# Memory rows transposed ahead of their scaling, and gate sums by triangle products, in a streaming encoder step

## The chip, the cores and the metric

The kernel runs on one core of a Trainium2 chip. The metric is the device time of one execution in microseconds (us). Engines are named as in the profile: PE (TensorE matmuls; PEld its weight loads), DVE (VectorE), ACT (ScalarE), POOL (GpSimd) and SP (SyncE, which here issues all the DMAs; SPq is its queue in the timeline).

## The reference

One inference step of a one-layer trunk in fp32: 1024 new frames of one stream and 16 new frames of each of 8 running streams, 1024 features. Three mixers run side by side on the normalised rows (stick-breaking attention, a Mamba-2 group, and forgetting attention), then cross-attention into 256 memory rows and a SwiGLU FFN. The change touches the memory rows' keys and values, and the running sums of the forget gates:

```python
def rmsnorm(x, g):
    xf = x.astype(jnp.float32)
    y = xf * lax.rsqrt(jnp.mean(xf * xf, axis=-1, keepdims=True) + EPS)
    return (y * g.astype(jnp.float32)).astype(x.dtype)

def mem_kv(mem, g, wk, wv):
    mn = rmsnorm(mem, g)
    k = jnp.einsum('bmd,de->bme', mn, wk) ...
    v = jnp.einsum('bmd,de->bme', mn, wv) ...

# in mixers(): new frames of the prompt, then of the running streams
logf = jax.nn.log_sigmoid((fg + p['fox_b_f']).astype(jnp.float32))
fcum = jnp.cumsum(logf, axis=1)
fcum = jnp.cumsum(jnp.concatenate([past['fox_logf'], logf], axis=1), axis=1)

# in fox_attend()
s = s + (fq[..., :, None] - fk[..., None, :])      # both are fcum
```

The cache holds 1024 past rows of four heads' log gates for each of 8 streams.

## The kernel before, in words

The program is written for a framework that orders the instructions of each engine by a simulated timeline and by priorities set in the code; each engine then runs its list in order, and a waiting instruction holds all that stand behind it on its engine. SP's DMAs take turns on eight semaphores, so that a DMA also waits for the one eight before it. Buffers come from pools: `st` for raw weights at the start, `ring` (tags `wh` and `wl`, three buffers each; `wr`, two) for weights, cached keys (`kf`) and cached values (`vr`).

Products keep fp32 accuracy by splitting each operand into a rounded high part and the rest: mm3 (L314 to L316) is high times high, high times low, low times high. A weight's high part is a cast on ACT (L289), the rest a subtraction in pieces of 256 columns on POOL (L132).

*The start.* L140 loads the 256 memory rows in two halves of 128x1024; L143 and L144 load six rows of gains, the convolution's bias and its taps, which PE turns into columns (L219). mem_proj (L783) normalises the memory rows by norm_T (L258): squares on ACT (L265), the root by rstd_of (L249 to L255, POOL and DVE), the scaling on DVE (L269), then eight times two transposes (L275), a copy to the high part with the gain (ACT, L276) and the low part (DVE, L277). Sixteen units of two 128x512 weight tiles of wk_x and wv_x follow, 12 products each; four units make one output, copied out on ACT (L804). Between the units come pieces of `aux`: norm_T for nine blocks of the x rows, with the same lines, from `ws` tiles.

*The gate sums.* fill_s (L1200) hands out work that fills PE's gaps while the stick-breaking pipeline runs: the last projections, then fox_sums (L646), pad_cols (transposes L756), and in the order `ORD` the first half of the z projection (products L314 to L316 of 264 columns), the convolution's columns, and z's second half. fox_sums stores the log gates (L650, L651), transposes the prompt's to rows (L657), scans 4x1024 (DVE, L659), stores the sums as `fcsc`, transposes them back (L663) into `fqc`. It gathers the cached gates (L669, 8192 runs of four floats), puts them in order (L672), transposes to rows (L678), adds the new frames' (L681, L685), scans 32x1040 (DVE, L687) and stores the rows 16 times over to DRAM as `fssc` (L688). L692 to L697 make `fnew`. Later the decode units of the forgetting attention read `fssc` back into `fkb` (L877), and four small loads (L1211, `fqs`) read the new frames' sums from it.

Beside this run the pipeline's rows (scores on PE L547 to L550; sigmoids on ACT L504 and L505 into `ws`; a scan on DVE, L507; a product on POOL, L132; transposes L565, copies to `pt` L568, products with values L580; the heads' output is stored to `mixsc` by L596) and the decode units: cached keys loaded (L851), transposed (L857), copied (L858), multiplied (L844), their weights transposed (L891, L892) and multiplied with the cached values (loads L909, products L900).

Of the kernel before, what the change touches and what calls it, by code (L numbers as in the profile page):

```python
# [62 lines left out]
def tile_hybrid_step(ctx: ExitStack, tc: tile.TileContext, a: dict):  # L63
# [22 lines left out]
    def act_t(dt=F32R, home=None):  # L86
        return (home or actp).tile([P, 3072], dt, tag="act", name="act")
# [4 lines left out]
    def st_t(dt=F32R):  # L92
        return stp.tile([P, 1024], dt, tag="st", name="st")
# [4 lines left out]
    def xc_t(dt=F32):  # L98
        return xcp.tile([P, 1056], dt, tag="xc", name="xc")
# [10 lines left out]
    def pd():  # L110
        return ps_t(psd, "d")
# [4 lines left out]
    def pT():  # L116
        return ps_t(pst, "t")
# [17 lines left out]
        return sm.tile([P, 16], dt, tag="sm", name="sm")[:, :n]  # L135


    xm = act_t(F32)
    for i in range(2):
        SP.dma_start(out=xm[:, i * D:(i + 1) * D], in_=a["mem_prompt"][0, i * P:(i + 1) * P, :])  # L140
    rows = xc_t()
    for i, g in enumerate(("norm_mix_g", "norm_x_g", "norm_ffn_g", "mem_norm_g", "conv_b")):
        SP.dma_start(out=rows[8 * i:8 * i + 8, :P], in_=a[g][0].rearrange("(k p) -> k p", p=P))  # L143
    SP.dma_start(out=rows[40:72, :P], in_=a["conv_w"][0].rearrange("i (k p) -> (i k) p", p=P))  # L144
    first_raw = []
    for k0 in (0, 2):
# [69 lines left out]


    colp = pT()
    PE.transpose(colp[:, :72], rows[:72, :P], ident[:72, :72])  # L219
    cols = cst.tile([P, 72], F32, name="cols")  # L220
    DVE.tensor_copy(cols, colp[:, :72])
    DVE.tensor_scalar(cols[:, 32:72], cols[:, 32:72], 0.5, None, ALU.mult)
    g_mix, g_x, g_ffn, g_mem = (cols[:, 8 * i:8 * i + 8] for i in range(4))
    conv_b = cols[:, 32:40]

    hb = mcst.tile([P, 28], F32, name="hb")
    lf = mcst.tile([P, NBLK, 4], F32, name="lf")
# [10 lines left out]
    mix_sc = dram([8, 2, P, T], F32R, "mixsc")  # L238
    o_sc = dram([8, 2, P, T], F32R, "osc")
    fc_sc = dram([4, SEQ], F32, "fcsc")  # L240
    fs_sc = dram([32, DEC_S, PAST + DEC_S], F32, "fssc")
    ac_sc = dram([72, P], F32, "acsc")
    mk_sc = dram([256, D], F32, "mksc")
    mv_sc = dram([256, D], F32, "mvsc")
# [401 lines left out]
    def fox_sums():  # L646
        l = log1p_exp_negabs(lf, [P, NBLK, 4])
        DVE.scalar_tensor_tensor(lf.rearrange("p a b -> p (a b)"), lf.rearrange("p a b -> p (a b)"), 0.0,
                                 l.rearrange("p a b -> p (a b)"), ALU.min, ALU.subtract)
        SP.dma_start(out=a["p_fox_logf"][0, 0].rearrange("(k p) h -> p k h", p=P), in_=lf[:, 0:8, :])  # L650
        SP.dma_start(out=a["s_fox_logf"][0].rearrange("b q h -> (b q) h"), in_=lf[:, 8, :])  # L651

        fr = xc_t()
        for hf in range(2):
            tp = pd()
            for b in range(4):
                PE.transpose(tp[:4, b * P:(b + 1) * P], lf[:, 4 * hf + b, :], ident)  # L657
            ACT.copy(fr[0:4, hf * 512:(hf + 1) * 512], tp[:4])
        DVE.tensor_tensor_scan(fr[0:4, :SEQ], fr[0:4, :SEQ], fr[0:4, :SEQ], 0.0, ALU.add, ALU.bypass)  # L659
        SP.dma_start(out=fc_sc, in_=fr[0:4, :SEQ])  # L660
        tp = pd()
        for b in range(8):
            PE.transpose(tp[:, b * 4:(b + 1) * 4], fr[0:4, b * P:(b + 1) * P], ident[:4, :4])  # L663
        DVE.tensor_copy(fqc, tp[:, :32].rearrange("p (b h) -> p b h", h=4))
        yield


        pl0 = sg_t()[:, :256]
        SP.dma_start(out=pl0.rearrange("p (u h) -> p u h", h=4),  # L669
                     in_=a["cache_fox_logf"][0].rearrange("b k h -> (b k) h").rearrange("(u p) h -> p u h", p=P))  # L670
        pl1 = sg_t()[:, :256]
        DVE.tensor_copy(pl1.rearrange("p (k b h) -> p k b h", k=8, h=4),  # L672
                        pl0.rearrange("p (b k h) -> p k b h", k=8, h=4))
        sr = xc_t()[0:32, :PAST + DEC_S]
        for hf in range(2):
            tp = pd()
            for b in range(4):
                PE.transpose(tp[:32, b * P:(b + 1) * P], pl1[:, (4 * hf + b) * 32:(4 * hf + b + 1) * 32], ident)  # L678
            ACT.copy(sr[:, hf * 512:(hf + 1) * 512], tp[:32])
        x8 = sg2_t()  # L680
        DVE.tensor_tensor(out=x8[:, :32].rearrange("p (b h) -> p b h", h=4),  # L681
                          in0=lf[:, 8, :].unsqueeze(1).to_broadcast([P, 8, 4]),
                          in1=smask.unsqueeze(2).to_broadcast([P, 8, 4]), op=ALU.mult)
        tp = pd()
        PE.matmul(tp[:32, :16], x8[:, :32], fold, start=True, stop=True)  # L685
        ACT.copy(sr[:, PAST:], tp[:32, :16])
        DVE.tensor_tensor_scan(sr, sr, sr, 0.0, ALU.add, ALU.bypass)  # L687
        SP.dma_start(out=fs_sc, in_=sr.unsqueeze(1).to_broadcast([32, DEC_S, PAST + DEC_S]))  # L688
        yield
# [93 lines left out]
    def mem_proj(xm, aux):  # L783

        mh, ml = act_pair(256)
        drain(norm_T([xm[:, i * D:(i + 1) * D] for i in range(2)], g_mem, lambda: (mh, ml), 256, xm[:, 2 * D:]))
        work = [(a[wname][0], j, k0, sc, out) for wname, sc, out in (("wk_x", mk_sc, "p_mem_k"), ("wv_x", mv_sc, "p_mem_v"))
                for j in range(2) for k0 in (0, 2, 4, 6)]
        nxt = [[t[:, :1024].rearrange("p (k n) -> p k n", n=512) for t in split_unit(raw, 1024)] for raw in first_raw]
        for n, (w, j, k0, sc, out) in enumerate(work):  # L790
            wh, wl = nxt.pop(0)
            if n + 2 < len(work) :
                w2, j2, k2 = work[n + 2][:3]
                nxt.append(w_unit([(w2, j2 * 512, 512)], k2, 2, st_t(F32)))
# [12 lines left out]
            next(aux, None)  # L807

    def decode_units(m):
# [15 lines left out]
        def rows(p):  # L827
# [372 lines left out]
    def fill_s():  # L1200
        yield from dense_T(w_in, uc, [(C_FQ, consume_qk(4, 0, QS))])
        yield from dense_T(w_in, uc, [(C_FQ + P, consume_qk(5, 1, QS))])
        yield from dense_T(w_in, uc, [(C_FK, consume_qk(6, 0, None, p_k[1], s_k[1]))])
        yield from dense_T(w_in, uc, [(C_FK + P, consume_qk(7, 1, None, p_k[1], s_k[1]))])
        yield from proj_v(1, C_FV, p_v[1], s_v[1], extra=4)
        yield from fox_sums()
        pad_cols()
        for o in ORD:
            if o == "z1":
                for p in range(4):  # L1210
                    SP.dma_start(out=fqs[:, p:p + 1], in_=fs_sc[8 * p:8 * p + 8, 0, PAST:PAST + DEC_S])  # L1211
# [777 lines left out]
```

## Time and profile before

| | |
|---|---|
| median of 3 runs | 1927.26 us (1920.28 to 1929.67) |
| the profiled execution's own time | 1923.12 us |
| its span in the trace | 1921.4 us |
| mean granted TensorE clock | 0.983 |
| PE busy | 1842.2 us |
| PE's waits in 0 to 76 us | 12.3 us |
| PE's waits in 270 to 335 us | 14.8 us |
| bytes moved by DMA | 307.52 MB |

The rows shown below are of five kinds. Waits: engine, tile and line that waited, what released it, us in total, times, longest. Timeline: start in us, duration, engine, line, operation, written tile, read tiles, shapes, and how often in a row; in brackets the idle time ahead of it and what ended it. Stretches: from and to, length, then busy time and instructions of PE, PEld, DVE, ACT and POOL, the granted clock, the DMA engines' busy share and GB/s. For SPq a timeline row's length is the time that the queue needed to hand the DMAs over, waits included. The page's head gives each engine's busy time and share of the span. The clock of a stretch is a record of the throttle.

### The profile page before, as it was taken

How to read it: one execution, taken by the hardware profiler on the slowest of the kernel's cores; microseconds unless marked ns; L12 is line 12 of the kernel's file. 1: busy time of each engine (PE TensorE's matmuls, PEld its weight loads, DVE VectorE, ACT ScalarE, POOL GpSimd, SP SyncE). 2: the span in 40 equal slices, each digit the busy share in tenths (PEclk: the TensorE clock that was granted, in tenths of full speed). 3: DMA queues.
4: the chain of work that ended last, by engine and by line, in shares of the span. 5: the costliest groups of instructions: out<-in, count | busy, mean ns of one | idle time of the engine just before them, and what ended most of it. 6: DMA issues, size and time to landing. Idle time of an engine off the chain costs nothing.

```text
span 1921.4 us, 32161 instructions
## 1 busy us (share of the span) xinstructions
PE 1842.2 (96%) x12128; PEld 1644.5 (86%) x12128; DVE 900.7 (47%) x1803; ACT 818.1 (43%) x1716; POOL 629.2 (33%) x915
## 2 busy tenths in 40 slices
PE   7989997989999899999999999999999999999998
PEld 5889776888986777899998889999999999888886
DVE  3421324365746883354435387333333433455555
ACT  6431543444656772243333175333333333344343
POOL 7632406154323663211101214554444443000000
PEclk9999996999999999999999999999999999999999
DMA  9454647445588887444558123322323223566572
GB/s 335 142 169 155 213 120 177 131 113 161 162 259 260 273 296 242 143 143 143 184 183 302 66 91 98 93 69 69 86 77 80 69 69 96 192 197 238 174 239 94
DMA packets 304778, 307.52 MB, mean 160 GB/s; under 512 B 88684, under 2 KB 259796, under 8 KB 304624
## 3 DMA queue, kind: packets, MB, share of 16 engines
q1 hardware_dynamic: 304624, 305.48, 51.5%
q8 instruction: 95, 1.56, 0.3%
q14 instruction: 59, 0.48, 0.1%
HBM read 229.31 MB, written 76.11 MB: 159 GB/s over the span
## 4 chain that ended last, share of the span: by engine, by line
PE 77%; DMA 7%; DVE 4%; POOL 3%; ACT 2%; issue 2%; SPq 1%; DVEq 0%; POOLq 0%; ACTq 0%
PE psd L1811 11%; PE psd L314 9%; PE psd L315 9%; PE psd L316 9%; PE pst L1811 8%; PE pss L1811 4%; PE pss L314 3%; PE pss L315 3%; PE pss L316 3%; DMA act<-acsc 2%; PE pso L1811 2%; PE pst L314 1%; PE pst L315 1%; PE pst L316 1%; PE pso L580 1%
## 5 line engine op out<-in xcount | busy, mean ns | idle before, releaser
L132 POOL TENSOR_TENSOR wl<-wr,wh 128x256 fp32r<-128x256 f32 (+1 forms) x180 | 139.0, 805 | 223.5 <-ACT wh L289 172.8
L314 PE MATMUL psd<-act,wh 128*128 128x384 f32 x576 | 198.0, 344 | 4.6 <-DVE sg L441 2.6
L316 PE MATMUL psd<-act,wl 128*128 128x384 f32 x576 | 196.7, 342 | 0.1
L315 PE MATMUL psd<-act,wh 128*128 128x384 f32 x576 | 196.2, 341 | 0.0
L1811 PE MATMUL pst<-bT,tr 128*128 128x256 f32 (+1 forms) x1068 | 155.0, 293 | 0.0
L1811 PEld LDWEIGHTS pst<-bT,tr 128*128 128x128 f32 x1068 | 144.9, 188 | 0.1
L316 PE MATMUL psd<-wh,act 128*128 128x512 f32 (+3 forms) x424 | 137.8, 326 | 0.0
L314 PE MATMUL psd<-wh,act 128*128 128x256 f32 (+3 forms) x414 | 134.9, 329 | 2.3 <-DMA act<-osc 1.1
L315 PE MATMUL psd<-wl,act 128*128 128x256 f32 (+3 forms) x414 | 135.2, 328 | 0.5 <-POOL wl L132 0.5
L1811 PE MATMUL psd<-bT,tr 128*128 128x320 f32 (+1 forms) x912 | 132.9, 295 | 0.7 <-DVE tr L1658 0.5
L1811 PEld LDWEIGHTS psd<-bT,tr 128*128 128x128 f32 x912 | 124.7, 188 | 1.2 <-DVE tr L1658 0.7
L132 POOL TENSOR_TENSOR ws<-ws 128x256 f32<-128x256 f32 (+2 forms) x100 | 74.3, 772 | 137.7 <-DVE ws L507 115.1
L314 PEld LDWEIGHTS psd<-act,wh 128*128 128x128 f32 x576 | 108.6, 188 | 10.7 <-DVE sg L441 3.0
L132 POOL TENSOR_TENSOR tr<-u,tr 128x256 fp32r<-128x256 f32 x110 | 83.3, 786 | 98.1 <-ACT tr L1654 80.3
L316 PEld LDWEIGHTS psd<-act,wl 128*128 128x128 f32 x576 | 108.4, 188 | 2.1 <-issue 1.5
L315 PEld LDWEIGHTS psd<-act,wh 128*128 128x128 f32 x576 | 108.6, 189 | 0.6 <-issue 0.4
L251 POOL TENSOR_SCALAR sm<-sm 128x1 f32<-128x1 f32 (+2 forms) x27 | 9.0, 335 | 300.2 <-ACT y L1894 209.4
L1786 DVE TENSOR_TENSOR tr<-tr,pst 128x256 f32<-128x256 f32 (+1 forms) x86 | 38.6, 449 | 138.2 <-ACT tr L1783 105.1
L132 POOL TENSOR_TENSOR tr<-raw,tr 128x256 fp32r<-128x256 f32 x94 | 69.3, 765 | 85.9 <-ACT tr L1654 77.7
L1654 ACT CAST tr<-tr 128x384 fp32r<-128x384 f32 (+1 forms) x70 | 37.7, 538 | 122.5 <-DMA tr<-hidsc 112.3
L314 PEld LDWEIGHTS psd<-wh,act 128*128 128x128 f32 x414 | 80.2, 194 | 10.6 <-issue 1.3
L289 ACT CAST wh<-wr 128x1024 fp32r<-128x1024 f32 (+2 forms) x45 | 46.7, 1050 | 97.6 <-PE psd L316 35.2
(609 smaller groups left out, 4713.2 us busy)
## 6 DMA issues: line engine op xcount, KB each, us to landing
u<-w_down SPq DMA_DIRECT2D x40, 512.0 KB
raw<-w_down SPq DMA_DIRECT2D x26, 512.0 KB
st<-qksc SPq DMA_DIRECT2D x48, 256.0 KB
wr<-w_in SPq DMA_DIRECT2D x22, 512.0 KB
tr<-hidsc SPq DMA_DIRECT2D x57, 192.0 KB
hidsc<-tr SPq DMA_DIRECT2D x34, 288.0 KB
qksc<-sg SPq DMA_DIRECT2D x48, 192.0 KB
wr<-cache_sb_k SPq DMA_DIRECT2D x16, 512.0 KB
```

The source lines that it names most:

```text
L132: POOL.tensor_tensor(out=out[:, a0:a1], in0=in0[:, a0:a1], in1=in1[:, a0:a1], op=op)
L251: POOL.tensor_scalar(v, ss, inv, EPS, ALU.mult, ALU.add)
L289: ACT.copy(hi[:, :n], raw[:, :n])
L314: PE.matmul(out, ah, bh, start=start, stop=False)
L315: PE.matmul(out, ah, bl, start=False, stop=False)
L316: PE.matmul(out, al, bh, start=False, stop=stop)
L580: return PE.matmul(po[r:r + 64, q_], vt[:, 2 * (k0 + i) + j, :], pfs[i][:, sl], start=start and k0 == 0 and (j == 0 or qp > 0), stop=k0 + ...
L1654: ACT.copy(hi, src)
L1786: DVE.tensor_tensor(out=at(out, g), in0=at(x, g), in1=ps[g][:, :GW[g]], op=op)
L1811: PE.matmul(dst[g][:, :GW[g]], x[:, ka], y[:, k, :], start=start and k == 0 and m == 0, stop=stop and k == 3 and m == 2, skip_group_check= ...
```

## The change

*Start.* The loads are put in the order memory half 1, five rows of gains and bias, first weights, memory half 2, three more weights, the taps. The memory rows are transposed as they are; the copies to the high and low parts apply the gain; squares and root are taken after the first unit, and the root scales the copy-out of each product (`ACT.activation(t, ps[i], AF.Copy, scale=...)`). The taps become columns after the second unit. Weights are loaded four units ahead instead of two. Units 0, 1, 2, 5, 8, 11 and 14 take their low part on DVE in one subtraction of 1024 columns instead of four on POOL.

*Gate sums.* Sums within a block of 128 rows are products with a triangle of ones, sums of earlier blocks products of running column sums (small additions on DVE) with a matrix of ones. The prompt's sums come out as columns (`fqc`) and are transposed to rows for `fcsc`; the cached ones come out as rows. A scan of 16 columns remains. `fssc` holds two copies instead of 16, and `fkb` reads each eight times.

*Order of the fqs loads.* They are kept in program order.

```diff
-    xm = act_t(F32)
-    for i in range(2):
+    xm, rows = act_t(F32), xc_t()
...
+    load_xm(0)
     for i, g in enumerate(("norm_mix_g", "norm_x_g", "norm_ffn_g", "mem_norm_g", "conv_b")):
         SP.dma_start(out=rows[8 * i:8 * i + 8, :P], in_=a[g][0].rearrange("(k p) -> k p", p=P))
...
+    load_wk(0)
+    load_xm(1)
+    for n in range(1, 4):
+        load_wk(n)
+    SP.dma_start(out=rows[64:96, :P], in_=a["conv_w"][0].rearrange("i (k p) -> (i k) p", p=P))
...
-    fs_sc = dram([32, DEC_S, PAST + DEC_S], F32, "fssc")
+    fs_sc = dram([32, 2, PAST + DEC_S], F32, "fssc")
...
+        pl0, pl1 = sg_t(), sg_t()
+        SP.dma_start(out=pl0[:, :256].rearrange("p (u h) -> p u h", h=4),
+                     in_=a["cache_fox_logf"][0].rearrange("b k h -> (b k) h").rearrange("(u p) h -> p u h", p=P))
+        triu, ones = pl1[:, 256:384], pl1[:, 384:512]
...
+        for b in range(1, 7):
+            DVE.tensor_tensor(out=pre[:, 4 * b + 4:4 * b + 8], in0=pre[:, 4 * b:4 * b + 4], in1=lf[:, b, :], op=ALU.add)
+        tp = pd()
+        PE.matmul(tp[:, :32], triu, lf[:, 0:8, :].rearrange("p b h -> p (b h)"), start=True, stop=False)
+        PE.matmul(tp[:, 4:32], ones, pre[:, 4:32], start=False, stop=True)
+        DVE.tensor_copy(fqc.rearrange("p b h -> p (b h)"), tp[:, :32])
...
-        DVE.tensor_tensor_scan(fr[0:4, :SEQ], fr[0:4, :SEQ], fr[0:4, :SEQ], 0.0, ALU.add, ALU.bypass)
...
-            PE.transpose(tp[:, b * 4:(b + 1) * 4], fr[0:4, b * P:(b + 1) * P], ident[:4, :4])
...
+                PE.matmul(o, pp[:, k * 32:(k + 1) * 32], triu, start=True, stop=k == 0)
+                if k:
+                    PE.matmul(o, ps_[:, k * 32:(k + 1) * 32], ones, start=False, stop=True)
...
-        DVE.tensor_tensor_scan(sr, sr, sr, 0.0, ALU.add, ALU.bypass)
-        SP.dma_start(out=fs_sc, in_=sr.unsqueeze(1).to_broadcast([32, DEC_S, PAST + DEC_S]))
-        yield
+        DVE.tensor_tensor_scan(n8, n8, n8, 0.0, ALU.add, ALU.bypass)
+        DVE.tensor_scalar(sr[:, PAST:], n8, sr[:, PAST - 1:PAST], None, ALU.add)
+        SP.dma_start(out=fs_sc, in_=sr.unsqueeze(1).to_broadcast([32, 2, PAST + DEC_S]))
...
-        drain(norm_T([xm[:, i * D:(i + 1) * D] for i in range(2)], g_mem, lambda: (mh, ml), 256, xm[:, 2 * D:]))
...
+                    for t in split_unit(first_raw.pop(0), 1024, DVE if n < 2 or n % 3 == 2 else POOL)]
...
+            ACT.activation(mh[:, k, :], tp[:, :256], AF.Copy, scale=g_mem[:, k:k + 1])
+            DVE.scalar_tensor_tensor(ml[:, k, :], tp[:, :256], g_mem[:, k:k + 1], f32(mh[:, k, :]), ALU.mult, ALU.subtract)
...
-                    ACT.copy(t, ps[i])
+                    ACT.activation(t, ps[i], AF.Copy, scale=rstd[0][:, i:i + 1])
...
+            if n == 0:
+                root()
+            if n == 1:
+                tap_columns()
...
-            SP.dma_start(out=fkb[:, :PAST], in_=fs_sc[8 * p:8 * p + 8, :, :PAST].rearrange("i t k -> (i t) k"))
+            SP.dma_start(out=fkb[:, :PAST],
+                         in_=fs_sc[8 * p:8 * p + 8, :, :PAST].rearrange("i c k -> (i c) k").unsqueeze(1)
+                         .to_broadcast([16, DEC_S // 2, PAST]))
...
-                    SP.dma_start(out=fqs[:, p:p + 1], in_=fs_sc[8 * p:8 * p + 8, 0, PAST:PAST + DEC_S])
+                    tc.keep_in_program_order(
+                        SP.dma_start(out=fqs[:, p:p + 1], in_=fs_sc[8 * p:8 * p + 8, 0, PAST:PAST + DEC_S]))
```

The change also moves instructions that it doesn't name. On SP, where the gate sums begin, before (L851 loads cached keys, L306 the z columns of w_in, L669 gathers the cached gates):

```order
L851 DMA wr<-cache_sb_k 128x1024 x2
L669 DMA sg<-cache_fox_logf 128x64x4
L596 DMA mixsc<-sg 64x2x256
L306 DMA wr<-w_in 128x4x256
L306 DMA wr<-w_in 128x4x8
L306 DMA wr<-w_in 128x4x256
L306 DMA wr<-w_in 128x4x8
L650 DMA p_fox_logf<-lf 128x8x4
L651 DMA s_fox_logf<-lf 128x4
```

and now (L668 is the gather, L910 the keys, L664 and L665 the stores of the gates, L320 w_in):

```order
L668 DMA sg<-cache_fox_logf 128x64x4
L910 DMA wr<-cache_sb_k 128x1024 x2
L610 DMA mixsc<-sg 64x2x256
L664 DMA p_fox_logf<-lf 128x8x4
L665 DMA s_fox_logf<-lf 128x4
L320 DMA wr<-w_in 128x4x256
L320 DMA wr<-w_in 128x4x8
L320 DMA wr<-w_in 128x4x256
L320 DMA wr<-w_in 128x4x8
```

The gather went from behind the two key loads to ahead of them, and the two stores of the gates from behind the w_in loads to ahead of them.

On ACT at the same place, before (L858 copies transposed keys, L568 transposed weights of the pipeline, L658 the gates' rows; L289 is the cast of w_in's z columns):

```order
L858 COPY kf<-pst 128x512 x4
L568 COPY pt<-pst 128x512 x2
L504 ACTIVATE ws<-pss 128x512
L505 ACTIVATE ws<-pss 128x512
L504 ACTIVATE ws<-pss 128x128
L505 ACTIVATE ws<-pss 128x128
L658 COPY xc<-psd 4x512 x2
L568 COPY pt<-pst 128x384
L289 CAST wh<-wr 128x1056
```

and now (L917, L582, L518, L519 and L303 are the former L858, L568, L504, L505 and L289; L693 copies the sums' rows):

```order
L917 COPY kf<-pst 128x512 x4
L303 CAST wh<-wr 128x1056
L582 COPY pt<-pst 128x512 x2
L693 COPY xc<-psd 4x512 x2
L303 CAST wh<-wr 128x1056
L518 ACTIVATE ws<-pss 128x512
L519 ACTIVATE ws<-pss 128x512
L518 ACTIVATE ws<-pss 128x128
L519 ACTIVATE ws<-pss 128x128
L582 COPY pt<-pst 128x384
```

Both casts went ahead, the first of them ahead of the copies of the pipeline's weights. POOL's list follows: both splits of w_in's z columns now stand ahead of the product of the decode unit's 1152-column row, which was ahead of the first and is now behind the second. On PE three score rows of the pipeline (256, 384 and 512 columns) went from ahead of the z projection to behind its first blocks.

On SP behind the sums' store, before (L688 stores `fssc`, L1211 the four `fqs` loads, L769 stores z, L909 loads cached values):

```order
L688 DMA fssc<-xc 512x1x1040
L851 DMA wr<-cache_sb_k 128x1024
L1211 DMA fqs<-fssc 128x1x1 x2
L769 DMA zsc<-sg 128x256
L1211 DMA fqs<-fssc 128x1x1 x2
L909 DMA vr<-cache_sb_v 128x1024 x2
```

and now:

```order
L720 DMA fssc<-xc 64x1x1040
L800 DMA zsc<-sg 128x256
L970 DMA vr<-cache_sb_v 128x1024 x2
L506 DMA st<-qksc 64x1024
L507 DMA st<-qksc 64x1024
```

The `fqs` loads are gone from here; they stand some 90 rows further on in SP's list. The key load went ahead of the store. Towards the out-projection a few instructions on each engine trade places; none is added there. From the cross-attention on, the lists are alike.

More of the change, by code (lines that the diff above doesn't have):

```diff
@@ L218, in tile_hybrid_step, with tap_columns @@
     colp = pT()
-    PE.transpose(colp[:, :72], rows[:72, :P], ident[:72, :72])
+    PE.transpose(colp[:, :40], rows[:40, :P], ident[:40, :40])
     cols = cst.tile([P, 72], F32, name="cols")
-    DVE.tensor_copy(cols, colp[:, :72])
-    DVE.tensor_scalar(cols[:, 32:72], cols[:, 32:72], 0.5, None, ALU.mult)
+    DVE.tensor_copy(cols[:, 0:40], colp[:, :40])
+    def tap_columns():
+        tp = pT()
+        PE.transpose(tp[:, :32], rows[64:96, :P], ident[64:96, 64:96])
+        DVE.tensor_copy(cols[:, 40:72], tp[:, :32])
+        DVE.tensor_scalar(cols[:, 32:72], cols[:, 32:72], 0.5, None, ALU.mult)
     g_mix, g_x, g_ffn, g_mem = (cols[:, 8 * i:8 * i + 8] for i in range(4))
@@ L226, in tile_hybrid_step @@
     hb = mcst.tile([P, 28], F32, name="hb")
+    xm_r = mcst.tile([P, 2], F32, name="xm_r")
     lf = mcst.tile([P, NBLK, 4], F32, name="lf")
@@ L656, in fox_sums @@
             for b in range(4):
-                PE.transpose(tp[:4, b * P:(b + 1) * P], lf[:, 4 * hf + b, :], ident)
+                PE.transpose(tp[:4, b * P:(b + 1) * P], fqc[:, 4 * hf + b, :], ident)
             ACT.copy(fr[0:4, hf * 512:(hf + 1) * 512], tp[:4])
-        DVE.tensor_tensor_scan(fr[0:4, :SEQ], fr[0:4, :SEQ], fr[0:4, :SEQ], 0.0, ALU.add, ALU.bypass)
         SP.dma_start(out=fc_sc, in_=fr[0:4, :SEQ])
[L661 to L664, printed above, removed]
-        yield
[L668 to L679, printed above, removed]
+        DVE.tensor_copy(ps_[:, 32:64], pp[:, 0:32])
+        for k in range(1, 7):
+            sl = slice(32 * k, 32 * k + 32)
+            DVE.tensor_tensor(out=ps_[:, 32 * k + 32:32 * k + 64], in0=ps_[:, sl], in1=pp[:, sl], op=ALU.add)
         x8 = sg2_t()
@@ L785, in mem_proj, with unit, root @@
         mh, ml = act_pair(256)
-        drain(norm_T([xm[:, i * D:(i + 1) * D] for i in range(2)], g_mem, lambda: (mh, ml), 256, xm[:, 2 * D:]))
         work = [(a[wname][0], j, k0, sc, out) for wname, sc, out in (("wk_x", mk_sc, "p_mem_k"), ("wv_x", mv_sc, "p_mem_v"))
                 for j in range(2) for k0 in (0, 2, 4, 6)]
-        nxt = [[t[:, :1024].rearrange("p (k n) -> p k n", n=512) for t in split_unit(raw, 1024)] for raw in first_raw]
+        def unit(n):
+            return [t[:, :1024].rearrange("p (k n) -> p k n", n=512)
+                    for t in split_unit(first_raw.pop(0), 1024, DVE if n < 2 or n % 3 == 2 else POOL)]
+        nxt = [unit(0)]
+        for k in range(KT):
+            tp = pT()
+            for i in range(2):
+                PE.transpose(tp[:, i * P:(i + 1) * P], xm[:, i * D + k * P:i * D + (k + 1) * P], ident)
+            ACT.activation(mh[:, k, :], tp[:, :256], AF.Copy, scale=g_mem[:, k:k + 1])
+            DVE.scalar_tensor_tensor(ml[:, k, :], tp[:, :256], g_mem[:, k:k + 1], f32(mh[:, k, :]), ALU.mult, ALU.subtract)
+        nxt.append(unit(1))
+        ss, rstd = small(2), []
+        def root():
+            for i in range(2):
+                ACT.activation(xm[:, 2 * D:], xm[:, i * D:(i + 1) * D], AF.Square, accum_out=ss[:, i:i + 1])
+            r = xm_r[:, 0:2]
+            DVE.tensor_copy(r, rstd_of(ss, 2, 1.0 / D))
+            rstd.append(r)
         for n, (w, j, k0, sc, out) in enumerate(work):
             wh, wl = nxt.pop(0)
-            if n + 2 < len(work) :
-                w2, j2, k2 = work[n + 2][:3]
-                nxt.append(w_unit([(w2, j2 * 512, 512)], k2, 2, st_t(F32)))
+            if n + 4 < len(work):
+                w2, j2, k2 = work[n + 4][:3]
+                first_raw.append(st_t(F32))
+                SP.dma_start(out=first_raw[-1].rearrange("p (k n) -> p k n", n=512),
+                             in_=w2[k2 * P:(k2 + 2) * P, j2 * 512:(j2 + 1) * 512].rearrange("(k p) n -> p k n", p=P))
+            if n + 2 < len(work):
+                nxt.append(unit(n + 2))
             if k0 == 0:
```

33 lines of the change are left out of this document (24 added, 9 removed).

## The prediction

> **What bounds the kernel now.** I read the page's head first, then PE's waits in the two places that the change touches, then the busy time by stretch there, and the timeline where a wait had to be explained.
>
> ```profile
> span 1921.4 us, 32161 instructions
> PE 1842.2 (96%) x12128; PEld 1644.5 (86%) x12128; DVE 900.7 (47%) x1803; ACT 818.1 (43%) x1716; POOL 629.2 (33%) x915
> ```
>
> PE is busy for 1842.2 of 1921.4 us, so only PE's idle time, and PE's work at a reduced clock, can be won. The profiled execution took 1923.12 us; the median of the three runs is 1927.26, 4.1 above it. I sum against 1923.12 and add 4.1. A difference under 0.5% (9.6 us) is about what a measurement of this kernel cannot tell from no change.
>
> PE's waits in 0 to 76 us, then in 270 to 335 us (total, times, longest):
>
> ```profile
> PE pst L219 <- DMA xc<-conv_w: 6.6, 1, 6.6
> PE pst L275 <- DVE act L269: 3.0, 2, 2.8
> PE pst L275 <- DVE act L277: 1.3, 2, 0.9
> PE pst L275 <- DVE ws L269: 0.9, 2, 0.5
> ```
>
> ```profile
> PE pss L547 <- ACT ws L505: 4.3, 1, 4.3
> PE pso L900 <- DMA vr<-cache_sb_v: 3.5, 1, 3.5
> PE pst L857 <- DMA wr<-cache_sb_k: 2.0, 2, 1.1
> PE psd L663 <- DVE xc L659: 1.7, 1, 1.7
> ...
> PE pss L547 <- ACT xc L686: 0.8, 1, 0.8
> PE pst L891 <- POOL ws L132: 0.7, 1, 0.7
> ```
>
> The start idles 11.8 us in these, the gate sums and the decode unit beside them some 13. The busy time by stretch (length, then PE, PEld, DVE, ACT, POOL, then granted clock, DMA share, GB/s) shows what those gaps draw after them:
>
> ```profile
> 28.00:72.00 44.00, 42.10 (x200) 33.30 (x200) 18.04 (x25) 30.37 (x46) 43.67 (x61) 1.00 0.63 226
> 293.40:313.90 20.50, 14.69 (x62) 12.49 (x60) 11.89 (x12) 7.34 (x18) 20.50 (x27) 0.50 0.85 203
> 313.90:324.20 10.30, 8.24 (x95) 7.59 (x93) 2.06 (x4) 1.90 (x5) 2.76 (x7) 1.00 0.63 181
> 324.20:334.40 10.20, 8.28 (x62) 7.73 (x63) 1.51 (x7) 2.99 (x6) 2.79 (x4) 0.50 0.59 160
> ```
>
> Behind the gaps PE ran at half clock twice, for 20.5 and 10.2 us; half of the busy time there was lost. POOL was saturated in 28 to 72 us and in 293.4 to 313.9.
>
> **The start.** Timeline, 0 to 14 us:
>
> ```profile
> 4.60 1.06 ACT L265 ACTIVATE act<-act 128x1024 f32<-128x1024 f32 x1 [2.54 <-DMA act<-mem_prompt]
> 5.96 1.06 ACT L265 ACTIVATE act<-act 128x1024 f32<-128x1024 f32 x1 [0.20 <-DMA act<-mem_prompt]
> 8.02 1.04 ACT L289 CAST wh<-st 128x1024 fp32r<-128x1024 f32 x1 [0.91 <-DMA st<-wk_x]
> 8.88 1.89 DVE L269 TENSOR_SCALAR act<-act,sm 128x1024 f32<-128x1024 f32 x2
> 11.87 0.80 PE L314 MATMUL psd<-wh,act 128*128 128x512 f32 x1
> ```
>
> The two halves of the memory rows were there by 4.60 and 5.96. Squares, root and DVE's scaling (to 10.77) stood between them and the transposes, and the first product came at 11.87. The change takes that chain out. The second half now lands behind one 512 KB weight load, which I estimate from 5.96 - 4.60 = 1.36 us: 7.3. Then comes a transpose, the copy on ACT (behind a 1.04 us cast, and perhaps one square of 1.06): first product between 8.3 and 9.7. I take 9.2, a gain of 2.7. Fewer waits for the transposes of the x rows, whose scaling stood in DVE's queue beside mem's (1.3 + 0.9, of which I take half), add 1.1. POOL gives 28 of its pieces to DVE. There a subtraction of 1024 columns costs between 0.95 (the scaling above, 1.89 for two) and four POOL pieces; DVE is busy 18.04 of 44 us, so 7 of them hide. The root's squares now run on ACT beside products, and hide unless the first eviction comes before them, 48 products later. Sum 3.8, as **-4**; -6 if the squares stay out of the way, 0 if ACT's order holds the copies.
>
> **The gate sums.** SP, ACT and PE, by the timeline:
>
> ```profile
> 276.27 1.15 SPq L851 DMA_DIRECT2D wr<-cache_sb_k  x2
> 277.46 0.43 SPq L669 DMA_DIRECT2D sg<-cache_fox_logf  x1
> 278.00 6.76 SPq L596 DMA_DIRECT2D mixsc<-sg  x1
> 285.19 2.10 SPq L306 DMA_DIRECT2D wr<-w_in  x4
> 287.34 0.52 SPq L650 DMA_DIRECT2D p_fox_logf<-lf  x1
> 287.90 2.21 SPq L651 DMA_DIRECT2D s_fox_logf<-lf  x1
> ```
>
> ```profile
> 280.30 1.06 PE L857 MATMUL pst<-ident,wr 128*128 128x128 f32 x8 [0.97 <-DMA wr<-cache_sb_k]
> 282.43 1.07 PE L857 MATMUL pst<-ident,wr 128*128 128x128 f32 x8 [1.07 <-DMA wr<-cache_sb_k]
> 287.18 1.08 PE L580 MATMUL pso<-pt,st 128*64 128x256 f32 x8
> 299.63 0.58 PE L547 MATMUL pss<-st 128*128 128x256 f32 x1 [0.78 <-ACT xc L686]
> 305.72 0.80 PE L547 MATMUL pss<-st 128*128 128x512 f32 x1 [4.34 <-ACT ws L505]
> 308.49 0.59 PE L314 MATMUL psd<-wh,act 128*128 128x264 f32 x1
> ```
>
> ```profile
> 289.47 1.07 ACT L289 CAST wh<-wr 128x1056 fp32r<-128x1056 f32 x1 [0.63 <-DMA wr<-w_in]
> ```
>
> ```profile
> 286.26 0.29 DVE L672 COPY sg<-sg 128x256 f32<-128x256 f32 x1 [4.09 <-DMA sg<-cache_fox_logf]
> ```
>
> Against it: the gather of 8192 runs of 16 B held SP's queue for 6.76 us, landing at 286.26; it now stands ahead of the two key loads. The last keys, at 282.43 now, come 3.8 later if both share the bytes (286.26), 2.3 if half of the hold is the keys' own bytes, 6.8 if the whole hold falls on them. And the two stores of L650 and L651 (0.52 + 2.21 = 2.7) now stand ahead of the w_in loads, whose cast ran at 289.47 and now comes at 292.2. The cast is now ahead of the two copies to pt in ACT's queue: pt is ready at 292.2 + 1.07 + 1.1 = 294.4, so PE's L580 moves from 287.18 to 294.4. That covers the late keys too.
>
> For it: from there to the z projection before took 308.49 - 287.18 = 21.3. Of this the waits of 1.7, 0.8, 0.7 and 4.3 are 7.5; the 4.3 belongs to a score row that the change moves behind z blocks, with two others whose products, from 299.63 to about 301.4, took 1.75 at half clock. The scan and its transposes back go, 15 products of 32x128 come; I set them equal. So z starts at 294.4 + 21.3 - 7.5 - 1.75 = 306.5, 2.0 earlier. POOL allows it: it splits both halves of w_in first, then its 1152-column product. The moved rows come back at 0.9, at full clock: **-1**, between -5 (keys and casts at once) and +6 (the hold falls on both).
>
> **The clock.** In these rows PE fell to half clock at 293.4 and 324.2, each behind idle time, and came back after steady work. [...]
>
> **The second stretch.** SP's timeline:
>
> ```profile
> 318.76 2.19 SPq L1211 DMA_DIRECT2D fqs<-fssc  x2
> 321.06 0.87 SPq L909 DMA_DIRECT2D vr<-cache_sb_v  x2
> ```
>
> ```profile
> SPq L1211 <- DMA fssc<-xc: 7.8, 1, 7.8
> ```
>
> ```profile
> 325.68 1.94 PE L900 MATMUL pso<-vr,st 128*32 128x128 f32 x32 [3.54 <-DMA vr<-cache_sb_v]
> ```
>
> The second values were queued behind the fqs loads, which waited 7.8 us for the 2080 KB store; they took 325.68 - 321.06 = 4.6 to land. Now the store is an eighth, and the fqs loads stand far behind. The values can start once their buffers are free; at the latest, I assume, when the first group of 32 products is done, 318.5. Landing at 323.1, they leave 1.0 of the 3.5: -2.5. A gap of 1.0 was harmless at 282.43, so the clock stays up, and half of 8.28 comes back: -4.1. Sum **-6.6**, between -7.6 (no wait) and -2 (the clock falls for another reason). The later fqs loads, and fkb read in eight copies, are used hundreds of us on: 0. So is a reordering of a few instructions at the out-projection, 0 ± 2.
>
> The sum is -4 - 1 - 6.6 = -11.6: 1911.5 for the profiled execution, **1915.7** on the median.
>
> **Rivals.**
> *The gather eats the gain.* Keys and w_in land late by the upper bounds, z starts 6 late: -4 + 6 - 6.6 = -4.6, 1922.7. For it: the 6.76 us hold; against: PE waited 7.5 there that go.
> *The values' wait stays.* Buffers, not the queue, hold them, the clock falls again: -4 - 1 - 2 = -7, 1920.3. For it: the same buffers serve z's weights; against: SP issued them within 0.1 us once the fqs loads were out.
> *All comes out well.* -5 - 5 - 7.6 = -17.6, 1909.7.
> *Nothing happens where it counts.* PE's 96% is elsewhere and the gaps only move: 0, 1927.3.
> *Slower: the gather as a plug.* The keys wait the whole hold, PE idles from 279.3 (0.97 ahead of 280.30) to 287 or so, the clock halves there instead of at 293.4, and all work to z runs at half. The hold brings the first keys from 280.3 to 287.1, 7.8 of idle time. Before, 308.49 - 279.3 = 29.2 held 9.5 of waits and so 19.7 of work, some 10 of it at full clock ahead of 293.4 and the other 10 at half. Now that is 20 + 10, less the moved 1.75; and the 7.5 of waits stay, because the copies and products behind the late keys are late in turn. z starts at 279.3 + 7.8 + 20 + 10 - 1.75 + 7.5 = 322.9, 14.4 late. With the start at -4 and the second stretch only at -2: +8.4, 1935.7. It decides from an idle time ahead of the keys that halves the clock (1.1 did not) and work behind it too broken to raise it again; above break-even it needs z more than 6 late with the second stretch lost.
>
> **How the numbers follow.** Forecast 0.45 (1912 to 1919), all well 0.12, gather 0.18, values 0.14, nothing 0.05, slower 0.06. The forecast is 1915.7. The line to "faster" is 1927.26 - 9.6 = 1917.6: all of the upside and nine tenths of the forecast's 0.45, with a little of the values' case, 0.54. Same: the remainder up to 1936.9, 0.42; slower 0.04, the upper part of the plug. The range leaves out the far side of the upside and most of the plug: 1907 to 1930.
>
> **What would show it.** Right: first product near 9; no wait on conv_w, on L659's scan or on the score row; PE's wait for cache_sb_v under 1.5 and granted clock 1.00 in the 10 us around it; z starting near 306.5 less the start's gain. The key transposes' wait should grow by about 4. Wrong: a wait over 5 us at the keys with clock 0.50 from there; a wait on cache_sb_v over 3; or the first product after 11.

## The result, and the profile after

| | before | after |
|---|---|---|
| median, same runs | 1924.97 us (1919.59 to 1929.67, 18 runs) | 1930.3 us (1924.78 to 1936.28, 18 runs) |
| the profiled execution's own span | 1921.4 us | 1928.6 us |
| mean granted clock | 0.983 | 0.985 |

The ratio is 1.0035, 95% interval 1.0025 to 1.0046: slower by 0.35%, some 6.7 us, where 0.6% faster was forecast. It is inside the 0.5% that I called no change, and just outside the range.

The head of the page after:

```profile
span 1928.6 us, 32192 instructions
PE 1845.8 (96%) x12147; PEld 1650.0 (86%) x12147; DVE 903.6 (47%) x1824; ACT 816.6 (42%) x1716; POOL 603.8 (31%) x889
```

PE's waits after, first in 0 to 76 us, then in 270 to 345 us:

```profile
PE pst L227 <- DMA xc<-conv_b: 5.6, 1, 5.6
PE pst L829 <- DMA act<-mem_prompt: 1.3, 1, 1.3
PE pss L328 <- ACT wh L303: 1.2, 1, 1.2
PE pst L289 <- DVE act L291: 1.1, 1, 1.1
PE psd L328 <- ACT act L830: 0.7, 1, 0.7
...
```

```profile
PE pst L916 <- DMA wr<-cache_sb_k: 6.5, 1, 6.5
PE pst L952 <- POOL ws L132: 3.8, 1, 3.8
PE pso L594 <- ACT pt L582: 1.5, 1, 1.5
...
PE pso L961 <- DMA vr<-cache_sb_v: 0.4, 1, 0.4
```

The waits on the taps, on L659's scan, on the score row and nearly all of the values' wait are gone. In their place stand 6.5 us for the keys and 3.8 for POOL. The stretches there, columns as before:

```profile
280.60:290.80 10.20, 4.78 (x24) 4.81 (x25) 3.71 (x24) 2.36 (x5) 0.60 (x2) 0.50 0.77 134
290.80:304.40 13.60, 9.93 (x83) 6.75 (x81) 4.66 (x3) 9.01 (x19) 9.55 (x12) 1.00 0.81 234
304.40:318.10 13.70, 12.01 (x54) 11.35 (x55) 5.54 (x9) 4.06 (x11) 9.33 (x19) 0.50 0.31 88
318.10:330.00 11.90, 10.38 (x130) 8.91 (x128) 3.39 (x6) 3.66 (x9) 2.40 (x4) 1.00 0.32 102
```

Half clock now comes at 280.6, in the wait for the keys, and again at 304.4, in the wait for POOL. The stretch behind the values' wait runs at full clock.

Where the time went is seen best when the same products are paired in the two traces: the start of each after, minus its start before. Positive is late.

| us in the trace of before | PE after stands |
|---|---|
| first product (11.87, now 9.65) | -2.2 |
| 100 | -2.2 |
| 260 | +0.1 |
| z starts (308.49, now 312.07) | +3.6 |
| 340 | -0.4 |
| 465 | +0.8 |
| 660 | +2.4 |
| 720 | +0.4 |
| 760 | +4.4 |
| 1100 | +6.3 |
| 1880 | +6.6 |

So the start won 2.2 us and lost it by 260; the gate sums lost 3.5 and the values' stretch gave 4.0 back; then, where I had put nothing, 4.0 were lost between 720 and 760 and another 1.9 up to 1100.

### The profile page after: what moved, and what is told of

It reads as the page before. It is cut to its first block, busy times and chain, and to the rows that moved or that the text cites. A ratio compares the mean times of both kernels' runs of the same rounds, so it can differ in the third digit from the quotient of the medians.

```text
span 1928.6 us, 32192 instructions
## 1 busy us (share of the span) xinstructions
PE 1845.8 (96%) x12147; PEld 1650.0 (86%) x12147; DVE 903.6 (47%) x1824; ACT 816.6 (42%) x1716; POOL 603.8 (31%) x889
## 4 chain that ended last, share of the span: by engine, by line
PE 77%; DMA 6%; DVE 4%; POOL 3%; ACT 2%; issue 2%; SPq 0%; DVEq 0%; POOLq 0%; ACTq 0%
PE psd L1873 11%; PE psd L328 9%; PE psd L329 9%; PE psd L330 9%; PE pst L1873 8%; PE pss L1873 4%; PE pss L328 3%; PE pss L329 3%; PE pss L330 3%; PE pso L1873 2%; POOL wl L132 2%; PE pst L328 1%; PE pst L329 1%; PE pst L330 1%; DMA act<-acsc 1%
## 5 line engine op out<-in xcount | busy, mean ns | idle before, releaser
L132 POOL TENSOR_TENSOR ws<-ws 128x256 f32<-128x256 f32 (+2 forms) x100 | 69.0, 719 | 133.2 <-DVE ws L521 121.9
L328 PEld LDWEIGHTS psd<-wh,act 128*128 128x128 f32 x414 | 79.6, 193 | 10.9 <-issue 1.3
L330 PEld LDWEIGHTS psd<-wh,act 128*128 128x128 f32 x424 | 81.1, 192 | 6.0 <-issue 0.4
```

What stands on the lines that cost most here:

```text
L132: POOL.tensor_tensor(out=out[:, a0:a1], in0=in0[:, a0:a1], in1=in1[:, a0:a1], op=op)
L328: PE.matmul(out, ah, bh, start=start, stop=False)
L330: PE.matmul(out, al, bh, start=False, stop=stop)
```

## The experiments

The theories as they stood. A: the cost is at places, the late keys and the order near the out-projection (690 to 765 us). B: the new gate sums cost, the start keeps its gain. Other rivals stand with each run. Medians of before differ from batch to batch (1921.47 to 1924.97), so each ratio is against before's own runs in the same batch and on the same chip. PE's place against before is given from the profiled executions, one of each kernel. These can lie well off the median: start_only's was the fastest of its twelve, 4.1 us under the median, and after_hb's the slowest, 6.2 over. So a place tells where one execution gained or lost, and the ratio tells what the kernel is worth.

**start_only: the start's edits alone.** All hunks of the start, with `fox_sums`, `fssc`, `fkb` and the fqs loads as before.

> The start alone; the gate sums and the fqs loads as before. Theory A (the order near the out-projection costs): the order of 690 to 765 us moves with the start, as in the changed kernel, so the 2.2 us won at the first product are lost there: 0 to +4 us against the kernel before, PE late by 2 or more across 690 to 765. Theory B (the gate sums cost, the start keeps its gain): -2 to -4 us. Theory C (the order costs nothing and only the places of the half-clock windows differ): -2 to +2, with half-clock windows at other places than in the changed kernel.

Measured 1926.28 us, ratio 1.0013 (1.0000 to 1.0027): theory A's side, with an interval that just touches no change. Between 720 and 760 it went from -5.1 to -2.6, as the changed kernel went from +0.4 to +4.4, and up to 1100 it drifted by 2.0 like that. The lists show that the start moves the order there: it is none of its own work, the scheduler's simulated times changed.

**sums_only: the gate sums alone.** All hunks of `fox_sums`, `fssc` and `fkb`, and nothing else.

> The gate sums alone (gather ahead of the keys, fssc of two copies); the start as before, the fqs loads not held in program order. Theory A: key wait about 6.5 us, z starts 3 to 4 us late, the wait for the values gets shorter since the store is an eighth: -1 to +2 us. Theory B: +3 to +6 us.

Measured 1919.07 us, ratio 0.9972 (0.9956 to 0.9987): faster than both theories had it, though the keys' wait is there:

```profile
PE pst L874 <- DMA wr<-cache_sb_k: 6.6, 1, 6.6
PE pst L910 <- POOL ws L132: 3.9, 1, 3.9
```

It stood at +2.7 by z and -2.7 at 340, so the gate stretch and the values together gain, without the fqs hold. And it went on to -6.5 by 465, which the changed kernel did not. Theory B is out: alone, the sums are the best part.

**fqs_only: the fqs loads held in program order, nothing else.**

```diff
-                    SP.dma_start(out=fqs[:, p:p + 1], ...)
+                    tc.keep_in_program_order(SP.dma_start(out=fqs[:, p:p + 1], ...))
```

> Only the fqs loads held in program order: nothing but SP's list and two rows of ACT's differ from the kernel before. Theory A and B: the second values no longer queue behind the 2080 KB store, wait of 3.5 us under 1.5, and the 10.2 us at half clock behind it go: -4 to -7 us. Theory D (the values' buffers or the store's own transfer hold them): wait 2 to 4 us, 0 to -2.

Measured 1920.71 us, ratio 0.9988 (0.9969 to 1.0007): unclear, and less than expected. The mechanism is there, in the waits and in the stretches of this kernel:

```profile
PE pso L900 <- DMA vr<-cache_sb_v: 1.8, 1, 1.8
```

```profile
326.00:329.50 3.50, 3.08 (x39) 2.63 (x40) 0.80 (x4) 1.64 (x4) 0.59 (x1) 0.51 0.17 23
329.50:340.00 10.50, 10.50 (x86) 9.17 (x85) 1.44 (x7) 4.24 (x11) 3.81 (x7) 1.00 0.50 137
```

The wait fell from 3.5 to 1.8 and the half-clock time behind it from 10.2 to about 3.5. PE gained 4.5 there, and lost 5.7 around 600 us, where this execution had two half-clock stretches of 6.8 us and that of before one of 3.4.

**sums_fqs: both of these.**

> Gate sums and fqs loads, start as before. Theory A: the stretch of the changed kernel without its start and its order near the out-projection: -2 to 0 us. Theory B: as the changed kernel or worse, +5 to +9. If the fqs loads bring their gain also beside the new sums, this is 2 us or more below sums_only.

Measured 1919.55 us, ratio 0.9975 (0.9957 to 0.9993), the same as sums_only: with the store at an eighth, the fqs loads no longer hold the values, and keeping them in order adds nothing. The two parts that win 5 us and the start that loses 2.5 would make about -2; the changed kernel is at +6.7. Each of these has an interval of 2 to 3.5 us to either side, so the 9 us between are rough; they are no part's own. The lists show what they could be: sums_only and sums_fqs also have a new order from 340 to 440 us, which the changed kernel does not have, and the changed kernel has the order near the out-projection.

**before_gap: an added tile.** The kernel before, with a tile that nothing uses:

```diff
     hb = mcst.tile([P, 28], F32, name="hb")
+    mcst.tile([P, 2], F32, name="gap")
```

> The kernel before with an unused tile of two columns behind hb: every engine's list is the same, but all tiles of the left pools lie 32 bytes further, as they do where xm_r is allocated. Theory L (the place in SBUF makes single matmuls a few ns longer): PE falls behind the kernel before by 1.5 to 2.0 us between 780 and 1100 us, evenly, without a wait, as start_only and the changed kernel do; +1.5 to +2.5 in all. Rival (the drift comes with the start's order of instructions): no drift, 0 us.

Measured 1927.56 us, ratio 1.0010 (0.9992 to 1.0029); the time alone can't tell it. The traces can. One product at 784 us and the first transposes of the FFN's factors at 1102, in before, here (one line further down in the code), and after:

```profile
784.15 0.39 PE L314 MATMUL pss<-ws,act 128*128 128x512 f32 x1
1101.70 1.47 PE L1707 MATMUL pst<-ident,st 128*128 128x128 f32 x12
```

```profile
786.27 0.39 PE L315 MATMUL pss<-ws,act 128*128 128x512 f32 x1
1105.18 1.47 PE L1708 MATMUL pst<-ident,st 128*128 128x128 f32 x12
```

```profile
788.73 0.39 PE L328 MATMUL pss<-ws,act 128*128 128x512 f32 x1
1108.02 1.47 PE L1769 MATMUL pst<-ident,st 128*128 128x128 f32 x12
```

From the one to the other: 317.55, 318.91 and 319.29. PE's only wait in between is for `osc`, in the same order of kernels:

```profile
PE psd L314 <- DMA act<-osc: 1.1, 1, 1.1
```

```profile
PE psd L315 <- DMA act<-osc: 0.4, 1, 0.4
```

```profile
PE psd L328 <- DMA act<-osc: 0.8, 1, 0.8
```

Without it 316.45, 318.51 and 318.49: 2.1 us more in before_gap and 2.0 in the changed kernel, with the same products; the granted clock of this stretch was 1.00 in before and in the changed kernel. Most single products come out between 6 ns shorter and 10 ns longer, on the mean 1 ns longer. In sums_only, which adds no such tile, nine products in ten take the same time to the nanosecond. The other traces bear it out: between these two products, without waits, the three kernels with such a tile (before_gap, start_only and the changed one) took 318.5 to 318.8 us, and the ten without it that ran at full clock there 315.5 to 316.9. So the added tile, `xm_r` in the changed kernel, cost 2 us here, or 0.65% of this stretch. Why it does was not shown: the traces hold no addresses, and the 32 bytes are my account of how the tiles are laid out.

**after_hb: the changed kernel without the added tile.**

```diff
-    hb = mcst.tile([P, 28], F32, name="hb")
-    xm_r = mcst.tile([P, 2], F32, name="xm_r")
+    hb = mcst.tile([P, 32], F32, name="hb")
+    xm_r = hb[:, 28:30]
```

> The changed kernel with xm_r in four unused columns of hb, so that no tile moves; the lists are those of the changed kernel. Theory L: the drift goes, about 2 us below the changed kernel, +4 to +5 against before. Rival: +6 to +8.

Measured 1926.95 us, ratio 1.0015 (0.9998 to 1.0032): down by 0.2% from 1.0035, as theory L has it, though the two intervals overlap. The drift is gone: PE stood at +6.8 at 780 and +7.5 at 1100, and 0.4 of that is a wait of its own. It still lost from +2.8 to +6.9 between 720 and 760.

**after_late: the gather behind the keys.** As after_hb, and

```diff
-        SP.dma_start(out=pl0[:, :256]..., in_=a["cache_fox_logf"]...)   (at the head of the new sums)
...
+        SP.dma_start(out=pl0[:, :256]..., in_=a["cache_fox_logf"]...)
         pp, ps_ = pl1[:, :256], pl0[:, 256:]
```

> As after_hb, with the gather issued behind fox_sums' first yield: it then stands behind both key loads and the first half of z's w_in, the stores of the gates behind w_in; and the scheduler leaves the order near the out-projection as it was in the kernel before. Theory A' (the gather ahead of the keys and the order near the out-projection are what the change pays): key wait 2 us, no half-clock stretch before 290, z starts 3 us or more earlier than before, nothing lost at 735 to 765: -6 to -11 us. Rival (the pays lie elsewhere, in the products of ones or where the clock's windows fall): -2 to +3.

Measured 1917.72 us, ratio 0.9965 (0.9949 to 0.9981): 6.7 us faster than before, and 0.5% below after_hb. SP's queue now:

```profile
274.30 1.15 SPq L910 DMA_DIRECT2D wr<-cache_sb_k  x2
...
280.42 0.93 SPq L320 DMA_DIRECT2D wr<-w_in  x2
281.46 0.45 SPq L682 DMA_DIRECT2D sg<-cache_fox_logf  x1
282.02 6.08 SPq L320 DMA_DIRECT2D wr<-w_in  x2
```

and its keys and z:

```profile
PE pst L916 <- DMA wr<-cache_sb_k: 1.1, 1, 1.1
```

```profile
305.58 0.59 PE L328 MATMUL psd<-wh,act 128*128 128x264 f32 x1
```

The gather holds the queue as ever, 6.08 us, but only the second half of w_in stands behind it. z starts 2.9 earlier than before. There was a half-clock stretch at 278, so that point of the expectation failed. The order near the out-projection is that of before, and nothing was lost there (-2.5 at 720, -2.4 at 760). The change does two things at once, the gather's place and the order; the trace has the first at some 2.7 us (from 260 to 340 this kernel gains 5.4, after_hb 2.7), the second at 4.1.

**after_dve2: fewer low parts on DVE.** As after_hb, gather still ahead of the keys, and

```diff
-  DVE if n < 2 or n % 3 == 2 else POOL
+  DVE if n < 2 else POOL
```

> As after_hb, with the low parts of units 2, 5, 8, 11 and 14 back on POOL: the gather still goes ahead of the keys, but from 340 to 440 us the scheduler now orders as in sums_only, and near the out-projection only a few rows still differ from the kernel before. Theory S (the order that the scheduler happens to give, not the parts' own work, makes the difference between the changed kernel and the sum of its parts): -4 to -8 us. Rival (the parts' own work collides): +2 to +6.

Measured 1916.35 us, ratio 0.9945 (0.9924 to 0.9967), theory S. This is the lowest ratio of the study, but from six runs, and its interval overlaps those of sums_only, after_late and after_pool; against the median of all of before's runs in this batch, 1922.72, it would be 0.9967, and after_late 0.9974. It still waits 6.2 us for the keys. The stretch from 340 to 465 is where it departs, from -7.4 to -9.3, where after_hb went from -2.8 to -2.2. PE's waits in 385 to 445 us, before, after and here:

```profile
PE pso L580 <- ACT pt L568: 3.6, 1, 3.6
PE pst L891 <- POOL ws L132: 1.7, 1, 1.7
```

```profile
PE pso L594 <- ACT pt L582: 3.5, 1, 3.5
PE pst L952 <- POOL ws L132: 1.7, 1, 1.7
```

```profile
PE psd L328 <- ACT xc L751: 1.9, 1, 1.9
```

So the kernel before has these waits too: this order wins something that the changed kernel leaves, and did not lose. And in 690 to 770 us the wait for the output rows that starts the out-projection, before, after and here:

```profile
PE psd L314 <- DMA ws<-mixsc: 1.5, 1, 1.5
```

```profile
PE psd L328 <- DMA ws<-mixsc: 3.3, 1, 3.3
```

```profile
PE psd L328 <- DMA ws<-mixsc: 1.1, 1, 1.1
```

Five subtractions of 1024 columns, in the first 72 us, set the order at 400 and 740 us: through the scheduler's simulated time, since nothing else of them is left there.

**start_dve2: the start alone, without both.** `xm_r` in `hb`, two low parts on DVE; every list behind about the first 80 us is that of before.

> The start alone, without the 32 bytes (xm_r in hb) and with only units 0 and 1 on DVE. The scheduler then leaves every list behind about 80 us as it was before, in the gate sums and near the out-projection too. Theory S: what start_only lost (+2.5 us) was the drift of 1.5 to 2 and the order near the out-projection, so this keeps its gain of 2 to 3 at the first products: -1.5 to -4 us. Rival (the start's gain is given back at the next wait for data, whatever the order): -1 to +1.

Measured 1922.06 us, ratio 0.9996 (0.9980 to 1.0013): the rival. PE stood at -2.0 at the first product, -0.7 at 100 and +1.8 at 260, then with gains and losses at -1.1 by the end. Freed of the order and the tile, the start is 0.8 us under before, with an interval from 3.8 under to 2.5 over: the 4 us of the forecast are outside it, a gain of 2 is not.

**best_late_fqs: after_dve2 with the gather late.**

> after_dve2 with the gather behind the keys, so after_late with only units 0 and 1 on DVE: keys at once, no reordering near the out-projection, but also none of the new order from 340 to 440 us that after_dve2 has. Theory S (order there is worth some 4 us, the late gather some 3): like after_late and after_dve2, -6 to -10 us. Rival (the gather is what counts): -10 to -13.

Measured 1919.13 us, ratio 0.9983 (0.9966 to 1.0001): under both expectations. It lies above after_late, from which it differs only in five low parts on POOL instead of DVE: no sign that this work costs anything on DVE. The two intervals overlap. Nor did the late gather bring anything beside after_dve2, whose order from 340 to 440 us is gone here. Why it is no better than after_late is open; its one execution lost 3.2 us at 740, behind a half-clock stretch that after_late did not have.

**best_l3: one more yield ahead of the gather.**

```diff
+        yield
         SP.dma_start(out=pl0[:, :256]..., in_=a["cache_fox_logf"]...)
```

> As best_late_fqs, with the gather and the cached sums one more step later in fill_s (one more yield ahead of the gather). No instruction is added or left out, but the scheduler's list on SP now differs in some 40 places between 200 and 500 from that of best_late_fqs. Theory S: differs from best_late_fqs by more than 3 us, either way. Rival (the work decides, not the order): within 2 us of best_late_fqs.

Measured 1918.4 us, ratio 0.9978 (0.9961 to 0.9995), within 1 us of best_late_fqs: the rival's number. By 400 its paired products stand some 13 us early, and by 1100 only 4.6: a different order need not mean a different end. The expectation of theory S fell here.

**after_pool: after_dve2's lists once more, all low parts of mem_proj on POOL.**

```diff
-  DVE if n < 2 else POOL
+  POOL
```

> As after_dve2, with units 0 and 1 on POOL too, so that no low part of mem_proj is on DVE. SP's list is that of after_dve2 to the last row, PE's differs in one place among the first 20. Theory S (the order from 270 us on makes after_dve2's gain): -6 to -11 us, the wait for the pt copies near 412 us gone again. Rival (after_dve2 was lucky, or DVE's first two low parts carry it): -4 to +1.

Measured 1918.24 us, ratio 0.9970 (0.9953 to 0.9987), 5.8 us: just short of theory S. The wait near 412 us is gone again, and PE stood at -6.7 both at 720 and at 760. Two kernels with this order are faster than before, two with the other (the changed kernel and after_hb) are not; all four have the same gate sums and the same gather ahead of the keys, and differ in how many low parts DVE takes.

## Why the prediction was wrong

**The start.** "First product 9.2, -2.7": it came at 9.65, -2.2, and the loads came as they were put. The two rows after:

```profile
8.04 0.90 PE L829 MATMUL pst<-ident,act 128*128 128x128 f32 x3 [1.29 <-DMA act<-mem_prompt]
9.65 0.80 PE L328 MATMUL psd<-wh,act 128*128 128x512 f32 x1 [0.70 <-ACT act L830]
```

The second half was waited for until 8.04, not 7.3. The 1.1 for the x rows' transposes did not come: PE stood at -2.2 at 100 us as well. So the term was about twice too large, and I booked it as a gain of the kernel without following it any further. In this execution it was gone by 260, up to 1.7 us of it to the clock. PE's waits in 100 to 128 us are alike in both traces (5.1 before, 5.4 after), but only after was a stretch at half rate drawn behind them. 127.0 to 130.4, before and after:

```profile
127.00:130.40 3.40, 3.02 (x18) 2.88 (x19) 2.17 (x3) 2.15 (x7) 1.37 (x2) 1.00 0.82 246
```

```profile
127.00:130.40 3.40, 3.40 (x12) 3.40 (x12) 1.28 (x2) 0.73 (x2) 1.83 (x4) 0.50 0.17 50
```

That stretch does not belong to the start. Of the fourteen traces eight have one between 126 and 135 us, among them fqs_only and sums_fqs, whose start is that of before. Where PE stood at 260 us, sorted by it:

| half clock between 126 and 135 us | start as before | new start |
|---|---|---|
| no | 0 (before), +0.3 (sums_only), +1.4 (before_gap) | -2.0 (after_late, after_dve2), -1.1 (best_late_fqs) |
| yes | +2.2 (fqs_only), +4.2 (sums_fqs) | -0.1 (after_hb), +0.1 (the changed kernel), +0.7 (after_pool), +1.8 (start_dve2, best_l3), +2.0 (start_only) |

On the mean the new start is some 2.2 us ahead in either row. So some 2 us of the 4 were there at 260, as an estimate from one execution of each kernel (other half-clock stretches are not sorted out), and that the changed kernel shows none was bad luck with the clock. Whether the 2 us reach the end, the medians can't tell.

**The gate sums.** "z starts 2.0 earlier, -1": it started 3.6 later. Three steps failed. First, the size of the keys' delay: I took 3.8 and kept 6.8 for the range; the gather's hold fell wholly on the key loads, and their transposes began 5.7 later (280.30, now 286.02):

```profile
276.37 0.44 SPq L668 DMA_DIRECT2D sg<-cache_fox_logf  x1
276.91 5.43 SPq L910 DMA_DIRECT2D wr<-cache_sb_k  x2
...
287.99 2.94 SPq L320 DMA_DIRECT2D wr<-w_in  x4
```

Second, w_in. I moved its cast by the two stores, 2.7; it went from 289.47 to 293.69, by 4.2. The issue went from 285.19 to 287.99, and not for the stores, which SP had handed over by 284.7. The reason is in SP's own waits:

```profile
SPq L320 <- PE pst L916: 2.1, 1, 2.1
...
SPq L320 <- DMA wr<-cache_sb_k: 1.2, 1, 1.2
```

w_in's raw tiles lie in the same two `wr` buffers as the keys, and so can't be loaded before the keys are transposed. Whoever delays one delays the other. Third, "POOL allows it": z's splits stood ahead of the 1152-column product, and PE's transposes of that product's weights, ahead of z in its list, waited 3.8 us for it. POOL, the splits and then the product:

```profile
294.85 8.19 POOL L132 TENSOR_TENSOR wl<-wr,wh 128x256 fp32r<-128x256 f32 x10 [12.03 <-ACT wh L303]
303.04 6.90 POOL L132 TENSOR_TENSOR ws<-ws 128x256 f32<-128x256 f32 x9
```

I had looked only at whether the splits come in time. after_late, with the keys first, has z at 305.58. That looks like the 306.5 that I had worked out for the changed kernel, but 2.0 of its 2.9 were there at 260 already, so that its gate stretch gave 0.9 of the 2.0.

**The second stretch.** "-6.6": PE went from +3.6 to -0.4, -4.0. The mechanism held at each step: the second values were issued at 322.25, as soon as the first 32 products were done at 322.2 (which I had assumed), the wait was 0.4, and the clock stayed at 1.00. Less came back because nine products of the three score rows that moved are in this stretch now (about 0.9 by my own sum, which I had booked by z), and two other waits there, for `so` and `ws`, came to 1.4 where before had 0.4. z itself ran at half clock no longer than before, 6.0 us against 5.4.

**The clock.** The last rival's first step came true: half clock came forward to 280.6, in the keys' wait. Its second did not: PE was back at full rate at 290.8, so the plug cost 3.5 us by z, not 14. The clock records of the two traces show how such stretches lie. From 20 to 1900 us before has seven at half clock, which begin at 293.40, 324.12, 412.87, 580.12, 638.15, 692.76 and 1153.56 and last 20.48, 10.24, 3.41, 3.41, 6.83, 6.83 and 6.83: each length is a multiple of 3.413 us, and so is the distance from the first to each of the others, to within 0.01 us. The same holds of the eight of the changed kernel (3.41 from 126.96, 10.24 from 280.56, 13.65 from 304.45, 3.41 from 413.68, 3.41 from 580.93, 10.24 from 635.54, 3.41 from 741.36 and 3.41 from 1161.19). So in each of these traces the stretches begin on a grid of 3.413 us, and not on the same one: counted from the first instruction it lies at 3.27 us of a period in before, at 0.66 in the changed kernel. There is one trace of each kernel, so none shows the same program twice.

In the period of the grid ahead of each of the two stretches of before in these rows, PE was without a product for 1.6 us (290.0 to 293.4) and for 2.0 (320.7 to 324.1). In the two traces, from 20 to 1900 us, half rate followed all 13 of the full-rate periods with 1.8 us of idle or more, 1 of the 5 with 1.6 to 1.8, and 1 of the 1048 with less. So what a wait cost in them hung on where the grid cut it. The like waits in 100 to 128 us put 1.9 us into one period in the changed kernel, and at most 1.7 in before. 3.4 us at half rate cost up to 1.7, so one execution can't show a part that is worth 2 us, and the medians can only just.

**The order near the out-projection.** "0 ± 2": it cost 4.0 in the changed kernel, 4.1 in after_hb and 2.5 in start_only, with a half-clock stretch of 3.4 us in each between 734 and 748, which makes up to 1.7 of it; of the eleven other traces only that of best_late_fqs has one there. It is the largest term that I had put at nothing. The order around 400 us, which the changed kernel lacks and sums_only has, is no loss against before. Together the two are what the lists offer for the 9 us between the parts and the whole, and both came from a scheduler that reordered work far from the edit.

**The added tile.** Not in the sum at all: 2.0.

**Put together.** The change was to win 11.6 us and lost 6.7. In the two profiled executions the start's -4 became 0; gate sums -1 became +3.5; second stretch -6.6 became -4.0; between 340 and 465 PE lost 1.2, around 600 another 1.6, with waits for `cache_fox_k` (2.0, before 0.5) and `xbcsc` (2.0, before 1.3), of which fqs_only has the first too; 2.0 came back by 720, since before had a half-clock stretch from 692.8 to 699.6 that after lacks; then the out-projection's 4.0 and the drift's 1.9. The chain of rivals had the gather's plug as the only way to a slower kernel. What made it slower was several smaller things: three terms that came out worse than forecast but within their bounds, the out-projection outside its ±2, and the added tile, which was not in the sum.

Open: why the products take longer beside the added tile; whether the start's 2 us reach the end; why best_late_fqs is not below after_late; and how much of after_dve2's 0.55% is its order and how much the luck of six runs (after_pool, with the same lists, has 0.30%).

## What to carry to other kernels

Where a scheduler orders the lists by simulated times, compare the whole lists of before and after, and price every stretch that moved, also those far from the edit; then try neutral variants of the edit, since among them the order may come out better, as in after_dve2. A gain of 2 us at the start of a kernel is worth little more than one half-clock stretch of these traces (3.4 us, which cost up to 1.7), so follow it through the next waits, and over several executions in which the clock fell alike. The gather of 8192 runs of 16 bytes held the DMA behind it on SP's queue for 6.76 us in before and 4.95 in the changed kernel, so price who stands behind such a DMA; moving it back was no clear gain by itself here (after_late won, best_late_fqs did not against after_dve2). A load's buffer belongs in the reckoning as much as its place in the queue: w_in waited 2.1 us for the transposes of the keys that held its `wr` buffer.

## What the runs showed of the hardware

With a tile of 128x2 added, the stretch from 784 to 1102 us took PE longer: without waits 318.51 us in before_gap, 0.65% more than the 316.45 of before, and 318.49 in the changed kernel, where after_hb, without the tile, took 316.9. The granted clock there was 1.00 in before and the changed kernel. The 4442 products of the FFN that pair between 1200 and 1900 us of before took the same time in the changed kernel to 0.05 ns on the mean. Behind the gather of 8192 runs of 16 bytes the next DMA took SP's queue 6.76 us in before (a store) and 4.95 in the changed kernel (a load of keys), and the one behind that 0.38 and 0.35; in after_late two loads of w_in took it 6.08 together. From 20 to 1900 us of before and the changed kernel half clock came in whole multiples of 3.413 us, and a full-rate period of that length with 1.8 us or more without a product was followed by half clock 13 times of 13.
